# Element-wise work of the RWKV stages moved from GpSimd to ScalarE and VectorE in a two-layer trunk

## The chip, the cores and the metric

One NeuronCore of one Trainium2 chip. The metric is the device time of one execution, in microseconds. The kernel before takes 2108.77 us, the median of 3 runs (2105.18 to 2111.51).

## The reference

A trunk of two layers on 512 latent tokens and 256 context tokens, 1024 features, fp32. Layer 0 mixes by attention in four head pairs (MLA) and, on the other half of its width, by an RWKV-7 scan over the tokens, forwards and backwards, in 8 heads of 64. Layer 1 mixes by a gated linear recurrence. After each mixer comes a layer norm, a squared-ReLU MLP and another layer norm; all are modulated by the condition. The part that the change touches is the RWKV half:

```python
f = f + mu * (centred_shift(f) - f)          # centred_shift: half the sum of both neighbours
r, k, v, wl, al, gl = jnp.split(f, RWKV_SPLIT, axis=-1)
decay = jnp.exp(-jnp.exp(-softplus(-(w0 + tanh(wl) @ w2)) - 0.5))     # per direction
a = sigmoid(a0 + al @ a2)
kk = k * k_k;  kk = kk * rsqrt(sum(kk * kk) + 1e-12)                  # per head
k_dir = k * (1 + (a - 1) * k_a)
# per token: sa = S kk;  S = S * decay - sa (kk a)^T + v k_dir^T;  y = S r
```

## The kernel before

The program is written in pieces, and a planner orders the instructions of each engine by a simulated timeline when the program is built; on the chip each engine then runs its list in order. All DMAs that matter here go through SyncE's queue.

**Feature stage (`mixer0_in`, L963).** The modulated input lies feature-major in SBUF, as a high and a low part; a product with 128 columns of the input weights takes three matmuls per 128 rows, over the spans `SPANS` of 512 latent and 256 context tokens, into one of two banks `mm` (`product`, L1098). The weights come by DMA and are split into high and low part by ScalarE (L130) and VectorE (L136). Of the projections, three (decay, a and gate) go first, in banks of their own (`first`, L1134); then, for four head pairs p, one of k, of r and of v. Each goes through the token mix (`shift`, L1113): ScalarE copies each span into a padded row `fp` (L1127), VectorE adds the two neighbours (L1120), GpSimd scales the middle by `mu1` (L1121), VectorE combines both by `mu2` (L1124, twice). `keys` (L1196) makes the normalised key: GpSimd scales by `k_k` (L1199), ScalarE squares, TensorE sums over a head. `turn_v` (L1212) turns v token-major (L1218).

`features` (L1222) makes the operands of one head pair and direction: ScalarE's tanh of decay (L1226) and a (L1231); GpSimd scales the decay (L1232); VectorE's scan gives the log decay (L1236, L1238); ScalarE's exponentials `eq` and `ek` (L1242, L1243); GpSimd makes `kd` (L1247), times k (L1248); VectorE makes the rows of `pq` and `bk` (L1252 to L1254, L1268), GpSimd one more of `bk` (L1269) and one column of `pq` (L1255). Its `rest` (L1256) multiplies A of every 64-token chunk on TensorE (L1264), into the banks `z0` and `z1`, and VectorE masks it into `at` (L1265). After both directions, `inverse` (L993) copies both `at` to DRAM (L997), reads back the 16 x 16 diagonal blocks by 16 DMAs (L1004), inverts them on VectorE (L1010, L1012), and sends them back by DMA (L1018, L1022); GpSimd clears the diagonal blocks of `at` with `offm` (L1024). `series` (L1026) builds the whole inverse from both by products (L1040, L1055) and VectorE (L1045, L1057). `bonus` (L1274) is a side product.

**Pass over the chunks (`rwkv`, L1324).** 12 steps for each of four head pairs, both directions side by side. `prep` (L1339) loads the operands of four steps and multiplies all token pairs (L1367); the result is masked into `st`: half of it by VectorE out of the bank (L1371), the other half, but for the first group, by a ScalarE copy (L1373) and a GpSimd mask (L1374). A step (`step`, L1395) has two links: products into `z` (L1404, L1406), GpSimd scales the state `rv` by the decay into `ds` (L1412), VectorE overwrites it by a copy out of `z` (L1414); then products (L1424) and VectorE's new state (L1426), outputs (L1428) and ScalarE's copy of them (L1429). TensorE gets pieces of attention (`mla`, L765) between the links, 1.4 us of them planned for each.

Then come the output product, the MLP and layer 1, dense products all.

Of the kernel before, what the change touches and what calls it, by code (L numbers as in the profile page):

```python
# [10 lines left out]
F32 = mybir.dt.float32  # L11
# [7 lines left out]
NL = 512  # L19
# [8 lines left out]
def run(*gens):  # L28
    """emits pieces of work in turn"""
    gens = list(gens)  # L30
    while gens:
        gens = [g for g in gens if next(g, gens) is not gens]


def weave(tc, dense, lead):
    """emits pieces of both in turn; a dense piece is not issued before the piece of lead that it follows"""
    for ins in lead:
        with tc.issue_after(ins.ins):
            next(dense, None)
    run(dense)  # L40


class Rows:
    """[128, n, T] of several tiles"""
# [9 lines left out]
class Kern:  # L54
# [28 lines left out]
    def dense(self, stk, wbufs=(2, 3), mmb=4):  # L83
        """pools of the phases with dense products: PSUM, weights, small rows"""
# [13 lines left out]
    def rows(self, stk):  # L98
        """token-major rows"""
# [8 lines left out]
    # ---- parameter vectors as per-partition columns  # L108
# [29 lines left out]
    def fill(self, n=1):  # L138
        """emits up to n pieces of work that other phases left for later"""
# [4 lines left out]
    def paced(self, gen):  # L144
        """a piece of work that is not issued before the product that was emitted last"""
# [3 lines left out]
    # ---- weights: raw column groups, then hi/lo column tiles  # L149
# [5 lines left out]
    def w_split(self, raw, hi_eng="act", lo_eng="dve"):  # L155
        """raw [128, kt, c] -> (hi, lo)"""
# [6 lines left out]
    def w_tiles(self, ap, group=128, eng=("act", "dve")):  # L163
        """yields (j, (hi, lo)) for 128-column tiles of ap [K, M]"""
# [9 lines left out]
    def mm3(self, out, st, mv, ks, first=True, last=True):  # L174
        """out += sum_k st_k^T mv_k over (hi, lo) pairs; st(k), mv(k) -> (hi, lo) APs"""
# [12 lines left out]
    # ---- adaLN modulation: columns [128, 48, 2]  # L188
# [48 lines left out]
    def mods_spare(self, l, order, tag="md", raws=None, tmp=None):  # L237
        """the same for 128-column blocks, with buffers of its own: fills gaps of the tensor engine; yields after each"""
# [51 lines left out]
    # pieces of the modulation: 0 sh1, 1 sc1, 2 g1, 3 sh2, 4 sc2, 5 g2  # L290
# [3 lines left out]
    def scale1(self, l, piece, name):  # L294
        """1 + scale, [128, 8, 2]"""
# [9 lines left out]
    def ln_affine(self, l, lnname, shp, scp, mod_l, name):  # L305
        """columns for h = xn*G + B with the modulation (shp, scp) of layer mod_l folded in"""
# [19 lines left out]
    def ln_turn(self, t, i, end):  # L326
        """token-major rows of token tile i up to feature row end, and their statistics"""
# [8 lines left out]
    def ln_stats(self, t, i):  # L336
        """token tile i: rows in PSUM, mean and variance, 1 / deviation"""
# [12 lines left out]
    def ln_stats_norm(self, t, i):  # L350
        """token tile i: returns normalised [128 tok, 1024] in SBUF"""
# [47 lines left out]
    # ---- squared-ReLU MLP; accumulates (g/alpha) * mlp(h) into t  # L399
    def mlp(self, l, t, hhi, hlo, halves, g2, after_half):  # L400
# [3 lines left out]
        for ch in range(4):  # L404
# [3 lines left out]
            if ch == 0:  # L408
                # the first half, while the second is normalised
# [31 lines left out]
    def mm_residual(self, t, m, a, b, st, mv, ks, g, ps=None):  # L441
        """t[:, m, a:b] += g[m] * (st^T mv)"""
# [10 lines left out]
    # ---- last layer norm, token-major, straight to the output  # L453
# [11 lines left out]
    # ---- tokens in, feature-major out  # L465
# [1233 lines left out]
```

## Time and profile before

| | us |
|---|---|
| median of 3 runs (lowest, highest) | 2108.77 (2105.18, 2111.51) |
| the profiled execution: span, first to last instruction | 2108.1 |
| TensorE busy, share of the span | 1937.9, 92% |
| VectorE busy | 1286.0, 61% |
| ScalarE busy | 815.3, 39% |
| GpSimd busy | 449.6, 21% |
| mean granted TensorE clock | 0.962 |

The profile is of one execution. A time of an engine counts only what it executes, not what it waits; a wait is put down to the instruction that ended last among those waited for. In the rows, PE is TensorE, PEld its weight loads, DVE VectorE, ACT ScalarE, POOL GpSimd; L12 is a line of the kernel, and buffer numbers are left out of the names. The granted clock is a share of full speed. Matmul durations overlap: one can start before the one ahead of it has ended.

### The profile page before, as it was taken

The page shows a single profiled execution, that of the slowest core. Times are in us where ns is not written, and L with a number is a line of the kernel's source. Part 1 is how long each engine was busy: PE and PEld are TensorE (multiplying, and loading weights), DVE is VectorE, ACT ScalarE, POOL GpSimd, SP SyncE. Part 2 cuts the span into 40 slices and gives each one's busy share as a digit, 9 for nine tenths or more (in the row PEclk, how much of TensorE's full clock was granted, in tenths as well). Part 3 has the DMA queues.
Part 4 walks back from the last instruction along what each step waited for, and adds up shares of the span by engine and source line. Part 5 has one row for each costly group of instructions (what it writes and reads, how often), then busy time and mean ns, then how long its engine had stood idle before and what let it go on. Part 6 is the DMA issues. An engine that isn't in the chain of part 4 may idle for free.

```text
span 2108.1 us, 39763 instructions
## 1 busy us (share of the span) xinstructions
PE 1937.9 (92%) x16130; PEld 1734.2 (82%) x16130; DVE 1286.0 (61%) x2524; ACT 815.3 (39%) x1413; POOL 449.6 (21%) x473
## 2 busy tenths in 40 slices
PE   7888788699999988999999999999978889999997
PEld 4666666577777768999999999998867779999997
DVE  4558767737666668774654333456799665444456
ACT  2344232434545443441231321334768444233242
POOL 0346544624535531000000000001244200000000
PEclk8999899789999998999999999999989999999999
DMA  9455534544423228332332222246421673333334
GB/s 345 131 172 180 139 107 128 174 121 117 124 64 92 77 72 243 91 90 80 100 87 84 61 60 61 69 126 179 112 71 45 182 219 97 94 95 96 100 101 141
DMA packets 429302, 249.19 MB, mean 118 GB/s; under 512 B 79376, under 2 KB 414144, under 8 KB 428992
## 3 DMA queue, kind: packets, MB, share of 16 engines
q1 hardware_dynamic: 428648, 245.55, 39.7%
q8 instruction: 127, 2.08, 0.4%
q0 software_dynamic: 288, 1.05, 0.1%
q14 instruction: 55, 0.45, 0.1%
q10 hardware_dynamic: 184, 0.06, 0.0%
HBM read 209.38 MB, written 36.44 MB: 117 GB/s over the span
## 4 chain that ended last, share of the span: by engine, by line
PE 66%; DVE 13%; DMA 7%; ACT 4%; issue 4%; SPq 3%; POOL 2%; DVEq 0%; ACTq 0%; POOLq 0%
PE mm L183 16%; PE mm L184 16%; PE mm L185 16%; SPq L1004 2%; DVE wlo L136 2%; PE tr L183 2%; DMA wraw<-in_l_mlp_w_dram 1%; PE tr L184 1%; PE tr L185 1%; PE mm L884 1%; PE g L1390 1%; PE mm L875 1%; ACT whi L130 1%; POOL fp L1121 1%; PE g L1367 1%
## 5 line engine op out<-in xcount | busy, mean ns | idle before, releaser
L183 PE MATMUL mm<-hhi,whi 128*128 128x384 f32 (+2 forms) x1504 | 489.4, 326 | 2.0 <-DVE msq L427 2.0
L184 PE MATMUL mm<-hlo,whi 128*128 128x384 f32 (+2 forms) x1504 | 485.0, 323 | 0.2 <-DVE hlo L396 0.2
L185 PE MATMUL mm<-hhi,wlo 128*128 128x384 f32 (+2 forms) x1504 | 484.5, 322 | 0.0
L130 ACT CAST whi<-wraw 128x1024 fp32r<-128x1024 f32 x216 | 226.3, 1049 | 552.5 <-PE mm L184 452.5
L183 PE MATMUL mm<-uhi,whi 128*128 128x384 f32 (+1 forms) x1280 | 400.4, 314 | 3.5 <-DVE t L450 3.0
L185 PE MATMUL mm<-uhi,wlo 128*128 128x384 f32 (+1 forms) x1280 | 399.8, 313 | 2.8 <-DVE wlo L136 2.8
L136 DVE TENSOR_TENSOR wlo<-wraw,whi 128x1024 fp32r<-128x1024 f32 x216 | 277.4, 1285 | 203.6 <-ACT whi L130 199.2
L184 PE MATMUL mm<-ulo,whi 128*128 128x384 f32 (+1 forms) x1280 | 399.0, 312 | 1.8 <-DVE ulo L136 1.8
L183 PEld LDWEIGHTS mm<-hhi,whi 128*128 128x128 f32 x1504 | 285.4, 190 | 15.6 <-issue 2.7
L184 PEld LDWEIGHTS mm<-hlo,whi 128*128 128x128 f32 x1504 | 285.2, 190 | 10.5 <-issue 0.8
L185 PEld LDWEIGHTS mm<-hhi,wlo 128*128 128x128 f32 x1504 | 284.8, 189 | 10.1
L183 PEld LDWEIGHTS mm<-uhi,whi 128*128 128x128 f32 x1280 | 244.7, 191 | 4.9 <-DVE t L450 3.2
L185 PEld LDWEIGHTS mm<-uhi,wlo 128*128 128x128 f32 x1280 | 244.2, 191 | 4.5 <-DVE wlo L136 4.1
L184 PEld LDWEIGHTS mm<-ulo,whi 128*128 128x128 f32 x1280 | 244.4, 191 | 2.6 <-DVE ulo L136 2.3
L450 DVE SCALAR_TENSOR_TENSOR t<-mm,g,t 128x256 f32<-128x256 f32 (+2 forms) x200 | 93.0, 481 | 224.7 <-PE mm L185 220.7
L347 POOL TENSOR_TENSOR lnrs<-lnrs,mhalf 128x1 f32<-128x1 f32 x20 | 10.8, 546 | 1005.1 <-DVE lnrs L346 1005.0
L1412 POOL TENSOR_SCALAR ds<-rv,rw_dd 64x64 f32<-64x64 f32 x176 | 84.3, 479 | 160.6 <-DVE rv L1426 150.6
L427 DVE SCALAR_TENSOR_TENSOR msq<-mm,mr 128x384 f32<-128x384 f32 (+1 forms) x128 | 62.4, 487 | 45.0 <-ACT mr L425 44.8
L425 ACT ACTIVATE mr<-mm 128x384 f32<-128x384 f32 (+1 forms) x128 | 55.5, 434 | 83.7 <-PE mm L185 83.7
L130 ACT CAST uhi<-msq 128x384 fp32r<-128x384 f32 (+1 forms) x128 | 58.6, 458 | 75.1 <-DVE msq L427 74.9
L136 DVE TENSOR_TENSOR ulo<-msq,uhi 128x384 fp32r<-128x384 f32 (+1 forms) x128 | 63.3, 495 | 32.3 <-ACT uhi L130 28.6
L1426 DVE SCALAR_TENSOR_TENSOR rv<-z,rw_dd,ds 64x64 f32<-64x64 f32 x176 | 49.6, 282 | 28.1 <-PE z L1424 23.3
(416 smaller groups left out, 3087.4 us busy)
## 6 DMA issues: line engine op xcount, KB each, us to landing
wraw<-in_l_mlp_w_dram SPq DMA_DIRECT2D x148, 512.0 KB
mraw<-in_l_mod_w_dram SPq DMA_DIRECT2D x48, 512.0 KB
wraw<-in_l_w_in_dram SPq DMA_DIRECT2D x36, 512.0 KB
wraw<-in_l_w_out_dram SPq DMA_DIRECT2D x32, 512.0 KB
mw<-in_l_mod_w_dram SPq DMA_DIRECT2D x16, 512.0 KB
wraw<-in_l_mod_w_dram SPq DMA_DIRECT2D x16, 512.0 KB
rw_bk<-pqbk SPq DMA_DIRECT2D x8, 768.0 KB
rw_pq<-pqbk SPq DMA_DIRECT2D x8, 768.0 KB
```

The source lines that it names most:

```text
L130: nc.scalar.copy(hi, src)
L136: e.tensor_tensor(out=lo, in0=src, in1=hi.bitcast(F32), op=ALU.subtract)
L183: nc.tensor.matmul(out, sh, mh, start=f, stop=False)
L184: nc.tensor.matmul(out, sh, ml, start=False, stop=False)
L185: ins = nc.tensor.matmul(out, sl, mh, start=False, stop=l)
L425: nc.scalar.activation(r, ps, AF.Relu)
L427: nc.vector.scalar_tensor_tensor(out=sq, in0=ps, scalar=0.0, in1=r, op0=ALU.max, op1=ALU.mult)
L450: nc.vector.scalar_tensor_tensor(out=t[:, m, x:y], in0=ps[:, x - a:y - a], scalar=g[:, m, s:s + 1], in1=t[:, m, x:y], op0=ALU.mult, op1=AL ...
L875: nc.tensor.transpose(ps[:, j * 128:(j + 1) * 128], p[:, (j0 + j) * 128:(j0 + j + 1) * 128], self.ident)
L1004: nc.sync.dma_start((X, tm)[d][q:q + 45:4, e], dat[r0:r0 + 16, 12 * d:12 * d + 12, 16 * b:16 * b + 16].rearrange("s n t -> n s t"))
L1412: P.tensor_scalar(out=ds[d][H[e]], in0=rv[H[e], i, e, :], scalar1=dn[H[e]], scalar2=None, op0=ALU.mult)
L1426: V.scalar_tensor_tensor(out=rn[H[e], e, :], in0=zu[d][H[e], 1], scalar=dn[H[e]], in1=ds[d][H[e]], op0=ALU.mult, op1=ALU.add)
```

## The change

- Token mix: ScalarE scales each span by `mu1` on its way out of the bank; VectorE then adds each neighbour out of the bank, one product-and-add per neighbour and span. The padded rows and GpSimd's scaling are gone.
- A: VectorE writes two masked copies out of the bank: `dg` (all of the triangle, for the copy to DRAM) and `at` (the off-diagonal blocks alone). GpSimd's mask is gone; the constant `offmask` now holds the sign and the triangle of each direction.
- The scalings of the key (`k_k`) and of `kd` go from GpSimd to ScalarE, the decay's scaling, the key product and one row of `bk` from GpSimd to VectorE.
- In the pass, all of the pair products are masked by VectorE out of the bank, and the state is scaled by ScalarE.
- Some small tiles share one, and three constants live in another pool.

```diff
-    off = (s // 16) != (t // 16)
+    off = np.stack([((s // 16) != (t // 16)) * np.where(m, -1.0, 0.0) for m in (s > t, t > s)], 1)
...
-        offm = cload(self.c0, self.C["offmask"], [128, 64], "offm")
+        goff = cload(self.tmp, self.C["offmask"], [128, 2, 64], "goff")
...
-            for d, at in enumerate(ats):
-                nc.sync.dma_start(dat[:, 12 * d:12 * d + 12], at)
+            for d, (_, dg) in enumerate(ats):
+                nc.sync.dma_start(dat[:, 12 * d:12 * d + 12], dg)
...
-            for at in ats:
-                P.tensor_tensor(out=at, in0=at, in1=offm.unsqueeze(1).to_broadcast([128, 12, 64]), op=ALU.mult)
...
-                    V.tensor_tensor(out=s[:, 0:FW - 2], in0=fp[:, 0:FW - 2], in1=fp[:, 2:FW], op=ALU.add)
-                    P.tensor_scalar(out=fp[:, 1:FW - 1], in0=fp[:, 1:FW - 1], scalar1=mu1[:, j:j + 1], scalar2=None, op0=ALU.mult)
-                    for a, b in SPANS:
-                        o = a + (2 if a else 0)
-                        V.scalar_tensor_tensor(out=out[:, a:b], in0=s[:, o:o + b - a], scalar=mu2[:, j:j + 1],
-                                               in1=fp[:, o + 1:o + 1 + b - a], op0=ALU.mult, op1=ALU.add)
+                def evac(ps, a, b):
+                    A.activation(out[:, a:b], ps, AF.Copy, scale=mu1[:, j:j + 1])
+                    n = b - a
+                    for o, i in ((1, 0), (0, 1)):
+                        V.scalar_tensor_tensor(out=out[:, a + o:b - i], in0=ps[:, i:n - o], scalar=mu2[:, j:j + 1],
+                                               in1=out[:, a + o:b - i], op0=ALU.mult, op1=ALU.add)
...
-                P.tensor_scalar(out=kx, in0=f, scalar1=cols["l0_rwkv_k_k"][:, p:p + 1], scalar2=None, op0=ALU.mult)
+                A.activation(kx, f, AF.Copy, scale=cols["l0_rwkv_k_k"][:, p:p + 1])
...
-                P.tensor_scalar(out=lamp[:, 1:T + 1], in0=lamp[:, 1:T + 1], scalar1=CDEC, scalar2=CDEC, op0=ALU.mult, op1=ALU.add)
+                V.tensor_scalar(out=lamp[:, 1:T + 1], in0=lamp[:, 1:T + 1], scalar1=CDEC, scalar2=CDEC, op0=ALU.mult, op1=ALU.add)
...
-                P.tensor_scalar(out=kd, in0=ta, scalar1=kah[:, p:p + 1], scalar2=kam[:, p:p + 1], op0=ALU.mult, op1=ALU.add)
-                P.tensor_tensor(out=kd, in0=kd, in1=k, op=ALU.mult)
+                A.activation(kd, ta, AF.Identity, scale=kah[:, p:p + 1], bias=kam[:, p:p + 1])
+                V.tensor_tensor(out=kd, in0=kd, in1=k, op=ALU.mult)
...
-                    at = isb("at", (128, 12, 64), 4)
+                    at, dg = isb("at", (128, 12, 64), 4), sb("dg", (128, 12, 64), 2)
...
-                        V.tensor_tensor(out=at[:, 6 * i:6 * i + 6], in0=ps, in1=gmask[:, d:d + 1, :].to_broadcast([128, 6, 64]), op=ALU.mult)
-                    return at
+                        for x, m in ((dg, gmask), (at, goff)):
+                            V.tensor_tensor(out=x[:, 6 * i:6 * i + 6], in0=ps, in1=m[:, d:d + 1, :].to_broadcast([128, 6, 64]), op=ALU.mult)
+                    return at, dg
...
-                P.tensor_tensor(out=bk[:, :, 1, :], in0=ch(kd), in1=ch(ek), op=ALU.mult)
+                V.tensor_tensor(out=bk[:, :, 1, :], in0=ch(kd), in1=ch(ek), op=ALU.mult)
...
-                if e or p + j == 0:
-                    V.tensor_tensor(out=st[h, :, e], in0=kp[h], in1=mk, op=ALU.mult)
-                else:
-                    A.copy(st[h, :, e], kp[h])
-                    P.tensor_tensor(out=st[h, :, e], in0=st[h, :, e], in1=mk, op=ALU.mult)
+                V.tensor_tensor(out=st[h, :, e], in0=kp[h], in1=mk, op=ALU.mult)
...
-                        P.tensor_scalar(out=ds[d][H[e]], in0=rv[H[e], i, e, :], scalar1=dn[H[e]], scalar2=None, op0=ALU.mult)
+                        A.activation(ds[d][H[e]], rv[H[e], i, e, :], AF.Copy, scale=dn[H[e]])
```

## Rows read from the trace of the kernel before

**Rows 1.** Stages: us, busy PE, PEld, DVE, ACT, POOL, granted clock, DMA share, GB/s.

```profile
50.00:430.00 380.00, 312.38 (x2984) 246.44 (x2984) 257.07 (x418) 143.12 (x242) 192.38 (x137) 0.91 0.50 145
...
430.00:770.00 340.00, 324.61 (x4140) 248.68 (x4142) 218.58 (x613) 163.39 (x406) 144.86 (x228) 0.99 0.34 95
...
820.00:2108.00 1288.00, 1227.30 (x8484) 1184.36 (x8482) 745.07 (x1330) 474.54 (x701) 98.34 (x78) 0.98 0.36 103
```

**Rows 2.** TensorE's waits from 50 to 430 us: total, times, longest.

```profile
PE g L1055 <- DVE vt L1057: 6.8, 5, 2.8
...
PE z L1424 <- ACT bt L1392: 4.3, 3, 2.8
```

**Rows 3.** TensorE's timeline: start, us, instruction, idle before and its releaser.

```profile
216.19 1.09 PE L1218 MATMUL mm<-ident,f_v 128*128 128x128 f32 x4 [8.25 <-ACT ek L1243]
...
284.55 0.87 PE L1218 MATMUL mm<-ident,f_v 128*128 128x128 f32 x3 [7.11 <-DVE f_v L1124]
...
353.13 1.12 PE L1264 MATMUL z<-pqbk,pqbk 64*64 64x64 f32 x16 [4.86 <-POOL pqbk L1255]
```

**Rows 4.** VectorE: two lines' durations (min/median/max ns), and its timeline.

```profile
L1254 DVE TENSOR_TENSOR pqbk<-f_kk,eq x8: 930/2554/2597, 122.0 to 350.4; 128x756 f32<-128x756 f32 x8
...
L136 DVE TENSOR_TENSOR wlo<-wraw,whi x216: 1193/1226/2884, 26.1 to 2093.0; 128x1024 fp32r<-128x1024 f32 x108
...
215.30 1.14 DVE L1124 SCALAR_TENSOR_TENSOR f_v<-sh,mu,fp 128x512 f32<-128x512 f32 x2
```

**Rows 5.** Timeline of GpSimd and ScalarE: start, us, instruction, idle before.

```profile
278.22 5.40 POOL L1121 TENSOR_SCALAR fp<-fp,mu 128x770 f32<-128x770 f32 x1 [3.19 <-DVE sh L1120]
...
338.96 0.48 ACT L1231 ACTIVATE ta<-z,a0h 128x256 f32<-128x256 f32 x1 [0.18 <-PE z L1175]
...
342.64 3.43 POOL L1024 TENSOR_TENSOR at<-at,ri_offm 128x768 f32<-128x768 f32 x1 [8.54 <-DMA dat<-at]
...
346.07 0.97 POOL L1247 TENSOR_SCALAR kd<-ta,kah,kam 128x768 f32<-128x768 f32 x1
```

**Rows 6.** GpSimd's groups by line: busy us, mean ns, idle before.

```profile
L1412 POOL TENSOR_SCALAR ds<-rv,rw_dd 64x64 f32<-64x64 f32 x176 | 84.3, 479 | 160.6 <-DVE rv L1426 150.6
...
L1121 POOL TENSOR_SCALAR fp<-fp,mu 128x770 f32<-128x770 f32 x15 | 43.2, 2880 | 55.2 <-DVE sh L1120 53.7 <-DVE modred L232 1.4
...
L1374 POOL TENSOR_TENSOR st<-st,gmask 64x512 f32<-64x512 f32 x22 | 28.6, 1305 | 22.5 <-ACT st L1373 21.4
```

**Rows 7.** Groups of VectorE and ScalarE that price what moves.

```profile
L1371 DVE TENSOR_TENSOR st<-g,gmask 64x512 f32<-64x512 f32 x26 | 17.7, 682 | 4.7 <-ACT st L1373 3.9
...
L1265 DVE TENSOR_TENSOR at<-z,ri_gmask 128x384 f32<-128x384 f32 x16 | 8.7, 551 | 2.8 <-PE z L1264 2.6
...
L754 DVE TENSOR_TENSOR ek<-ek,eq 128x768 f32<-128x768 f32 x2 | 1.9, 955 | 1.4 <-ACT ek L750 1.4
...
L1188 DVE TENSOR_SCALAR ta<-ta 128x768 f32<-128x768 f32 x1 | 0.6, 556 | 0.0
...
L1429 ACT COPY ys<-z 128x64 f32<-128x64 f32 x96 | 20.2, 216 | 46.5 <-PE z L1428 42.5 <-DVE p L865 1.8 <-DVE bt L1379 1.4
...
L1373 ACT COPY st<-g 64x512 f32<-64x512 f32 x22 | 12.8, 581 | 11.6 <-PE g L1367 5.7 <-issue 2.2 <-POOL st L1374 1.4
...
L1226 ACT ACTIVATE lamp<-tr,w0h 128x768 f32<-128x768 f32 x8 | 7.2, 904 | 3.1 <-PE tr L1175 3.1
...
L1242 ACT ACTIVATE eq<-ek 128x768 f32<-128x768 f32 x8 | 6.8, 846 | 29.1 <-DVE ek L1238 17.8 <-DVE ek L1236 11.3
```

**Rows 8.** The stage table again, for four short windows.

```profile
210.00:220.00 10.00, 3.78 (x11) 2.97 (x12) 9.84 (x13) 5.09 (x10) 7.43 (x3) 0.55 0.43 129
...
280.00:290.00 10.00, 4.73 (x15) 3.70 (x16) 8.76 (x10) 5.57 (x11) 9.05 (x5) 0.52 0.31 54
...
350.00:360.00 10.00, 6.16 (x54) 4.67 (x55) 7.56 (x8) 4.42 (x7) 6.07 (x4) 0.55 0.59 127
...
394.00:430.00 36.00, 25.68 (x203) 19.67 (x205) 26.90 (x64) 11.03 (x25) 24.23 (x34) 0.65 0.70 195
```

More of the change, by code (lines that the diff above doesn't have):

```diff
@@ L980, in cload @@
         def cload(pool, src, shape, name):
-            t = pool.tile(shape, F32, name="ri_" + name)
+            t = pool.tile(shape, F32, name="ri_" + name, bufs=1)
             nc.sync.dma_start(t, src)
@@ L1022, in inverse @@
                         nc.sync.dma_start(dst[r0:r0 + 16, :, 16 * b:16 * b + 16], dx[e, :, b].rearrange("n s t -> s n t"))
-            for at in ats:
-                P.tensor_tensor(out=at, in0=at, in1=offm.unsqueeze(1).to_broadcast([128, 12, 64]), op=ALU.mult)
         def series(p, ats):
+            ats = [at for at, _ in ats]
             vts = [isb("vt", (128, 12, 64), 2) for d in range(2)]
@@ L1068, in mixer0_in @@
             col = lambda n, name: ri.tile([128, n], F32, name=name)
-            mu1, mu2, eps = col(15, "mu1"), col(15, "mu2"), col(1, "kkeps")
+            small = col(56, "small")
+            mu1, mu2, w0h, a0h, kah, kam, eps = (small[:, a:b] for a, b in zip((0, 15, 30, 38, 46, 50, 54), (15, 30, 38, 46, 50, 54, 55)))
             V.tensor_scalar(out=mu1, in0=mu, scalar1=-1.0, scalar2=1.0, op0=ALU.mult, op1=ALU.add)
@@ L1077, in mixer0_in @@
             V.tensor_scalar(out=kam, in0=kah, scalar1=-1.0, scalar2=1.0, op0=ALU.mult, op1=ALU.add)
-            fps = [col(FW, f"fp{i}") for i in range(2)]
-            for fp in fps:
-                for a, n in ((0, 1), (NL + 1, 2), (FW - 1, 1)):
-                    P.memset(fp[:, a:a + n], 0.0)
             lamp = col(T + 2, "lamp")
@@ L1086, in mixer0_in @@
             low = {n: [ri.tile([128, T], F32R, name=f"x{n}{d}") for d in range(2)] for n in ("w2", "a2")}
-            sh = lambda: sb("sh", (128, FW), 2)
+            sh = lambda: sb("sh", (128, T), 2)
             def wide(mm):
@@ L1113, in shift @@
             def shift(j, out):
-                fp = fps[nt[0] % 2]
-                nt[0] += 1
-                def mix():
-                    s = sh()
-                    V.tensor_tensor(out=s[:, 0:FW - 2], in0=fp[:, 0:FW - 2], in1=fp[:, 2:FW], op=ALU.add)
-                    P.tensor_scalar(out=fp[:, 1:FW - 1], in0=fp[:, 1:FW - 1], scalar1=mu1[:, j:j + 1], scalar2=None, op0=ALU.mult)
-                    for a, b in SPANS:
-                        o = a + (2 if a else 0)
-                        V.scalar_tensor_tensor(out=out[:, a:b], in0=s[:, o:o + b - a], scalar=mu2[:, j:j + 1],
-                                               in1=fp[:, o + 1:o + 1 + b - a], op0=ALU.mult, op1=ALU.add)
-                return (lambda ps, a, b: A.copy(fp[:, a + 1 + (2 if a else 0):b + 1 + (2 if a else 0)], ps)), mix
+                def evac(ps, a, b):
[4 more added lines that the diff above has]
+                                               in1=out[:, a + o:b - i], op0=ALU.mult, op1=ALU.add)
+                return evac
             def project(j, out):
-                evac, mix = shift(j, out)
-                yield from product(self.w_raw(w[:, W0 + 128 * j:W0 + 128 * j + 128], 8, 128), evac)
-                mix()
+                yield from product(self.w_raw(w[:, W0 + 128 * j:W0 + 128 * j + 128], 8, 128), shift(j, out))
             def first(js, outs):
@@ L1143, in first @@
                             self.mm3(o, lambda k: (wh[:, k, :], wl[:, k, :]), lambda k: (hhi[:, k, a:b], hlo[:, k, a:b]), [k], k == 0, k == 7)
-                for (evac, mix), pp in zip(after, ps):
+                for evac, pp in zip(after, ps):
                     for o, (a, b) in zip(pp, SPANS):
                         evac(o, a, b)
-                    mix()
                     yield
```

7 lines of the change are left out of this document (3 added, 4 removed).

## The prediction

> **What bounds the kernel now.** First the stretches [rows 1]. TensorE works 324.6 of the 340 us in which attention and the pass over the chunks run together, and 1227.3 of the last 1288 us, the dense layers that the change leaves alone. In the feature stage (50 to 430 us) it works 312.4 of 380 us: 67.6 us idle, 17.8%, at a granted clock of 0.91. GpSimd is busy 192.4 us there, VectorE 257.1. So a change to element-wise work can pay in that stage alone; in the pass, TensorE's idle share is 15.4 of 340, 4.5%.
>
> Next, which waits ended last for TensorE there [rows 2, 3]. Three gaps stand out. At 216.19 the transposes of v (L1218) start after 8.25 us, at 284.55 after 7.11 us, and at 353.13 the products for A (L1264) after 4.86 us. The rest are waits for the series (L1055) and for the first steps of the pass (L1424).
>
> Then what stood behind them. In the first two, v comes out of the token mix: VectorE adds the neighbours, GpSimd scales (L1121), VectorE combines (L1124). At 278.22 GpSimd took 5.40 us over the scaling, where L1121 needs 2.88 on average [rows 5, 6], and v followed it. For the first gap the row names ScalarE, but v's combination started at 215.30 [rows 4], which ends where the transposes begin: I read v as the releaser. In the third, ScalarE had the tanh for k's scaling ready at 339.44 (338.96 + 0.48), but GpSimd, which works in order, was held by the off-diagonal mask of the previous A (L1024) until the copy of that A to DRAM let go at 342.64; the mask ended at 346.07, and only then came kd (L1247), the key product and the decayed key [rows 5]. That is 6.6 us lost in one queue.
>
> The two engines also slow each other. L1254, the same VectorE product eight times, takes 930 ns at best and 2554 ns as median; the split of the weights (L136) 1226 ns as median and up to 2884 [rows 4].
>
> **The change, part by part.** TensorE's work is the same, and no DMA is added or taken away: the copy to DRAM reads the diagonal copy of A from a tile of its own. So the sum is over TensorE's idle time and its clock.
>
> *Token mix.* For each of 15 projections one GpSimd scaling (2880 ns, 43.2 us in all [rows 6]) and one VectorE addition go; ScalarE scales as it empties the bank, and VectorE adds each neighbour out of the bank. VectorE keeps about the same load: one SBUF addition and two combinations become four half-length combinations; a 512-column one out of PSUM should cost 0.68 us, as L1371 does [rows 7]. What goes is the hop to GpSimd and back. First gap: 8.25 us; the scaling's 3 us and the contention in front of it go, but the next weights still have to be split before the next projection, so I take 5.0 (bounds 0 and 8.25). Second gap: 7.11 us, of which GpSimd's 5.40 went wholly into the wait; I take 4.8 (bounds 0 and 7.11).
>
> *Masks of A, scalings and key products.* kd moves to ScalarE (0.90 us, as L1226 with a column operand), and the wait behind the DRAM copy is gone: 6.6 us in that chain against a gap of 4.86. I take 4.2 (bounds 0 and 4.86). The first key scaling (L1199) also goes to ScalarE, 4 passes at 0.85 to 0.90; it lies beside other work, and without that cover costs at most 3.6 us.
>
> *The clock after the gaps.* In the 10 us windows around the three gaps the granted clock was 0.55, 0.52 and 0.55 [rows 8], between the levels of 2.4 and 1.2 GHz; a mean of 0.55 puts 0.9 of the time at the lower one. That costs half of 0.9 x 3.78, 0.96 x 4.73 and 0.9 x 6.16 us of busy time: 1.7, 2.3 and 2.8, together 6.8. With the gaps cut to about a third, I take 4.5 back.
>
> *The start of the pass.* From 394 to 430 us TensorE is idle 10.3 us, at clock 0.65, with GpSimd busy 24.2 of 36 [rows 8]. The mask of the pair products (L1374) and the state scaling (L1412) leave GpSimd; the copies of the shared key and of the weights stay. I take half of the idle time, 5 (bounds 0 and 10.3, and up to 9 of clock: 0.7 x 25.68 / 2).
>
> *What VectorE pays.* New on it in the feature stage: 8 decay scalings at 0.556 us (L1188) = 4.4; 16 products at 0.955 (L754) = 15.3; 16 second masks at 0.551 (L1265) = 8.8; together 28.5 [rows 7]. Back come at least four L1254 at 2554 - 930 ns = 6.5. Net at most 22 us on an engine that is busy 257 of 380. Where this lands I can't see; weighted with TensorE's idle share it costs 22 x 0.178 = 3.9 (bounds 0 and 22).
>
> *The bank held longer.* No row shows a bank that waits for VectorE after a projection. Before, ScalarE alone emptied it; now two VectorE passes follow, 2 x 0.68 us plus their place in VectorE's queue. There are two banks, and the other one's products run meanwhile. Nearest is the feature stage's own idle share, so I take 1.5 us in all; bounds 0, and 36 (second rival).
>
> *The pass.* 176 state scalings (L1412, 84.3 us) leave GpSimd for ScalarE at about 0.216 us, the 128x64 copy's price: 38.0. 22 copies (L1373) at 0.581 go: 12.8. Net +25.2 on ScalarE; VectorE gains 22 masks at 0.682 = 15.0 and GpSimd loses 112.9 [rows 6, 7]. What queues behind a waiting scaling on ScalarE are the exponentials and copies of attention; TensorE waits for those. At TensorE's idle share of 4.5% the 40.2 us cost 1.8 (bounds -3, as the scalings were on the chain of steps too, and 8).
> The rows have 846 ns for a ScalarE pass with constants (L1242) and 904 for one with a column operand (L1226), equally long [rows 7]. The Trainium skill, *ScalarE: Activation LUTs*, section *What ACT_TABLE_LOAD costs*, puts 186 ns + 0.833 ns per element on a pass and about 93 ns on each column operand. The trace agrees in direction, with 58 ns. An estimate by that page is 332 ns for a scaling: 45.6 us net on ScalarE instead of 25.2, and 2.7 us in place of 1.8.
>
> **Sum.** -5.0 - 4.8 - 4.2 - 4.5 - 5.0 + 3.9 + 1.5 + 1.8 = -16.3 us. The profiled execution's span is 2108.1 us; the median of three runs is 2108.77, and the span lies within 0.7 of it. 2108.77 - 16.3 = 2092.5; I say **2092**.
>
> **The rivals.**
> A, *larger gain* (20%): the three gaps close wholly (20.2), their clock comes back (6.8), and the start of the pass loses its idle time and its low clock (19.3): 46 us, 2062. For it: the whole of the feature chain speeds up where both engines block each other now. Against: the inverse's many small DMAs and the series on VectorE stay, and fixed dates follow from them.
>
> B, *the hop goes, the time does not* (15%): VectorE becomes the bound of the feature stage. It is busy 9.84 and 8.76 of 10 us in the first two gap windows [rows 8]; with 22 us more, v's combination waits behind splits and masks instead of behind GpSimd. The gains of 23.5 are paid back by the 22 us: about 2107. The change then does what it says, and the gaps keep their length under another name.
>
> C, *slower* (12%): the two projection banks wait for VectorE. Three projections go first, in banks of their own; 12 remain, with two spans each: 24 evacuations. If a bank comes free 1.5 us too late each time, that is 36 us; -16.3 - 1.5 + 36 = +18, 2127. It decides from about 0.7 us each (16.3 + 1.5 over 24). For it: VectorE's queue is that full in [rows 8], and TensorE issues in order, so a late bank holds everything. Against: in these windows VectorE was full because of slowed instructions and of waits for GpSimd, which go.
>
> **How the numbers follow.** My forecast has 53%, A 20%, B 15%, C 12%. About 0.3%, 6.3 us, is what a measurement of this kernel tells from no change. Forecast and A are faster: 0.73; B is the same: 0.15; C slower: 0.12. The range, 2060 to 2114, takes in A and B and leaves out C's full price and what lies beyond A. The forecast alone, with the bounds of its gap terms, spans about 2078 to 2104.
>
> **What the changed profile would show.** Right: from 50 to 430 us GpSimd is busy under 149 us (192.4 less L1121's 43.2 alone), TensorE's idle time there is down by some 15 us, the wait of L1218 for v is a few us in all, and no wait of L1264 names a GpSimd product of 5 us; the pass begins some 15 us earlier and is as long as before. VectorE's L1254 sits near 0.93 us. Wrong: projections that wait for a VectorE addition (C); VectorE above 280 us in the stage with the gaps still there (B); or a pass longer than before with ScalarE named ahead of VectorE's state copies, which would put the cost of the state scalings far above my 1.8.

## The result and the profile after

The changed kernel takes 2123.59 us, the median of 8 runs (2116.98 to 2126.77), against 2109.77 for the kernel before, run beside it: a ratio of 1.0065, with a 95% interval of [1.0047, 1.0082]. One of the eight executions of the kernel before took 3421.4 us and is left out. The changed kernel is slower, where the prediction said 2092 and faster. The profiled execution (span 2115.9 us, mean granted clock 0.953) is one of its quicker ones, at 2117.68 us.

What was meant to go went. The stage table of the changed kernel (columns as in [rows 1]):

```profile
50.00:430.00 380.00, 316.24 (x3028) 250.06 (x3026) 248.02 (x475) 159.89 (x265) 50.82 (x61) 0.88 0.50 145
430.00:770.00 340.00, 316.51 (x3940) 243.06 (x3940) 219.96 (x599) 192.24 (x510) 44.70 (x54) 0.96 0.35 99
```

GpSimd's 192.4 us of the feature stage became 50.8, and VectorE, which got more to do, is busy 9 us less. But TensorE's idle time there fell by 3.9 us only (67.6 to 63.8), and its clock fell from 0.91 to 0.88. In the pass TensorE's busy time went down and its clock too. Four finer stretches show where, first of the kernel before, then of the changed one:

```profile
50.00:200.00 150.00, 134.70 (x889) 103.76 (x888) 93.51 (x136) 62.81 (x105) 71.71 (x40) 0.99 0.54 169
200.00:300.00 100.00, 76.67 (x841) 62.16 (x840) 77.62 (x132) 31.67 (x57) 56.52 (x32) 0.88 0.43 119
300.00:440.00 140.00, 111.00 (x1411) 88.62 (x1406) 88.77 (x161) 51.09 (x88) 65.91 (x69) 0.84 0.49 133
440.00:780.00 340.00, 322.03 (x4087) 245.53 (x4082) 222.83 (x628) 164.50 (x416) 145.74 (x230) 0.99 0.33 93
```

```profile
50.00:200.00 150.00, 128.27 (x807) 98.18 (x806) 87.49 (x157) 63.14 (x100) 7.67 (x12) 0.91 0.50 156
200.00:300.00 100.00, 91.77 (x896) 72.24 (x894) 77.84 (x160) 48.56 (x81) 10.48 (x13) 0.93 0.50 144
300.00:440.00 140.00, 106.20 (x1453) 87.72 (x1453) 86.71 (x169) 53.15 (x98) 34.15 (x42) 0.82 0.49 132
440.00:780.00 340.00, 315.01 (x3906) 241.53 (x3907) 222.20 (x607) 195.88 (x521) 43.22 (x48) 0.96 0.35 97
```

Width less PE busy is the idle time. From 200 to 300 us it fell from 23.3 to 8.2 us: both gaps of [rows 3] that lie there closed, and TensorE does not wait for the transposes of v in these 100 us. From 50 to 200 us it rose from 15.3 to 21.7 and the clock fell from 0.99 to 0.91; from 300 to 440 us it rose from 29.0 to 33.8; in the pass from 18.0 to 25.0, with the clock from 0.99 to 0.96. Over the 730 us that is 85.6 before and 88.7 after. Busy time times (1 - clock), a rough price of the lower level, makes 32 us before and 50 after (28 and 37 of these to 440 us).

TensorE's longest waits of the changed kernel from 50 to 430 us (total, times, longest):

```profile
PE g L1039 <- DVE vt L1044: 12.2, 3, 5.2
PE mm L1205 <- DVE f_k L1114: 7.1, 1, 7.1
PE mm L1039 <- DMA tau<-dx: 6.3, 1, 6.3
```

The first row is the series, which waited before too [rows 2]; the third is the last inverse's transfer. L1205 is the transposing of v, L1218 before. It does not wait for v now: it waits for f_k, another projection, whose bank it needs. VectorE's timeline around it, and TensorE's row:

```profile
177.22 0.74 DVE L1114 SCALAR_TENSOR_TENSOR f_k<-mm,small,f_k 128x511 f32<-128x511 f32 x1
179.50 0.61 DVE L1006 COPY X<-tm 48x512 f32<-48x512 f32 x1 [1.54 <-DMA tm<-dat]
180.14 1.76 DVE L1223 TENSOR_TENSOR_SCAN ek<-lamp,ri_reset 128x768 f32<-128x768 f32 x1
181.81 0.73 DVE L1114 SCALAR_TENSOR_TENSOR f_k<-mm,small,f_k 128x511 f32<-128x511 f32 x1
```

```profile
182.69 0.88 PE L1205 MATMUL mm<-ident,f_v 128*128 128x128 f32 x3 [7.08 <-DVE f_k L1114]
```

The first neighbour is added at 177.22. The second stands in VectorE's order behind the copy that opens the inverse (L1006), which waits for a DMA until 179.50, and behind a scan. From the end of the first addition (177.96) to the start of the second are 3.85 us, of which VectorE idles 1.54 for the DMA; the rest is the copy and the scan. The bank comes free at 182.54 (181.81 + 0.73), and 0.15 us later TensorE goes on, after 7.08 us. From 180 to 185 us its granted clock is 0.50, the level of 1.2 GHz, and 0.52 from 185 to 190. It is 0.50 as well from 320 to 325 us, after the series' longest wait (5.2), and from 420 to 430, after the wait for the transfer (6.3).

The pass starts earlier and lasts longer. The copies of its outputs, first and last start (before; after):

```profile
L1429 ACT COPY ys<-z x96: 191/212/253, 420.4 to 785.2; 128x64 f32<-128x64 f32 x96
```

```profile
L1413 ACT COPY ys<-z x96: 188/213/246, 409.6 to 801.5; 128x64 f32<-128x64 f32 x96
```

So 364.8 us became 391.9. The first eight copies alone take 60.1 us where they took 43.3 (the ninth starts at 469.7; before, at 463.7): the lead of 10.8 us is gone there. In these 60.1 us lie TensorE's 6.3 us of waiting for the last inverse's transfer (tau). The output product starts at 814.05 in place of 795.10. Of these 19 us, 11 come back by the end of this execution; where, was not followed.

Another price that was far off, that of the state scaling (first and last start again):

```profile
L1396 ACT ACTIVATE ds<-rv,rw_dd x176: 333/344/357, 402.6 to 792.4; 64x64 f32<-64x64 f32 x176
```

The state scaling takes 345 ns as a mean (60.7 us in 176), not the 216 of the copy row in [rows 7].
The estimate by the Trainium skill, *ScalarE: Activation LUTs*, section *What ACT_TABLE_LOAD costs*, was 332 ns; this row agrees with it within 4%.

### The profile page after: what moved, and what is told of

The parts are those of the page before. It is cut to its first block, busy times and chain, and to the rows that moved or that the text cites. A ratio compares the mean times of both kernels' runs of the same rounds, so it can differ in the third digit from the quotient of the medians.

```text
span 2115.9 us, 39567 instructions
## 1 busy us (share of the span) xinstructions
PE 1941.6 (92%) x16130; PEld 1738.2 (82%) x16130; DVE 1287.3 (61%) x2601; ACT 876.0 (41%) x1579; POOL 205.8 (10%) x210
## 4 chain that ended last, share of the span: by engine, by line
PE 66%; DVE 14%; DMA 6%; ACT 5%; issue 5%; SPq 3%; POOL 0%; DVEq 0%; ACTq 0%; POOLq 0%
PE mm L183 17%; PE mm L184 17%; PE mm L185 16%; DVE wlo L136 3%; SPq L1004 2%; DMA wraw<-in_l_w_out_dram 1%; PE tr L183 1%; DVE cy L592 1%; PE mm L875 1%; DMA wraw<-in_l_mlp_w_dram 1%; PE tr L185 1%; PE mm L884 1%; PE tr L184 1%; ACT whi L130 1%; DVE gx L644 1%
## 5 line engine op out<-in xcount | busy, mean ns | idle before, releaser
L184 PEld LDWEIGHTS mm<-hlo,whi 128*128 128x128 f32 x1504 | 287.3, 191 | 10.8 <-DVE hlo L396 0.5
L347 POOL TENSOR_TENSOR lnrs<-lnrs,mhalf 128x1 f32<-128x1 f32 x20 | 10.8, 548 | 996.6 <-DVE lnrs L346 961.2
L1396 ACT ACTIVATE ds<-rv,rw_dd 64x64 f32<-64x64 f32 x176 | 60.7, 345 | 25.8 <-DVE rv L1410 22.4
L276 DVE SCALAR_TENSOR_TENSOR macc<-mraw,sc,macc 128x128 f32<-128x128 f32 x224 | 67.6, 360 | 0.0
```

The source lines that it names most:

```text
L184: nc.tensor.matmul(out, sh, ml, start=False, stop=False)
L276: V.scalar_tensor_tensor(out=a, in0=raw[:, k], scalar=self.sc[:, k, i:i + 1], in1=a, op0=ALU.mult, op1=ALU.add)
L1396: A.activation(ds[d][H[e]], rv[H[e], i, e, :], AF.Copy, scale=dn[H[e]])
```

## The experiments

Each ratio is to the kernel before, run beside it on the same chip; the brackets are its 95% interval. "Feature edits" are the token mix, the masks of A, the scalings and the key products; "pass edits" are the state scalings on ScalarE and the pair masks on VectorE.

### Which half of the change

Four kernels undo or isolate the pass edits. The first has the feature edits alone:

```diff
-  A.activation(ds[d][H[e]], rv[H[e], i, e, :], AF.Copy, scale=dn[H[e]])
+  P.tensor_scalar(out=ds[d][H[e]], in0=rv[H[e], i, e, :], scalar1=dn[H[e]], scalar2=None, op0=ALU.mult)
...
-  V.tensor_tensor(out=st[h, :, e], in0=kp[h], in1=mk, op=ALU.mult)
+  if e or p + j == 0:
+      V.tensor_tensor(out=st[h, :, e], in0=kp[h], in1=mk, op=ALU.mult)
+  else:
+      A.copy(st[h, :, e], kp[h])
+      P.tensor_tensor(out=st[h, :, e], in0=st[h, :, e], in1=mk, op=ALU.mult)
```

> The changed kernel with both edits of the pass undone (state scalings on GpSimd, half of the pair products masked by GpSimd after a ScalarE copy); the feature stage stays changed. Theory P (the pass lost the time: 403.6 us from its first to its last state product where it was 382.2): the pass is back at 380 to 385 us and the whole runs 4 to 10 us below the kernel before. Theory F (the feature stage's new order and the banks held by VectorE lost it, and the pass only inherits a bad start): the whole stays 8 us or more above the kernel before.

Measured: 1.0073 [1.0046, 1.0100], median 2117.9 us; its profiled execution, at 2111.38, is its quickest one.

The changed kernel with the first replacement alone (state scalings back on GpSimd):

> The changed kernel with the state scalings alone back on GpSimd. Theory P1 (the scalings on ScalarE are what stretches the pass, 176 of them at 345 ns in a queue that attention waits for): the pass is below 387 us and the whole within 5 us of the kernel before, or below it. Theory P2 (the masks that moved to VectorE stretch it): the pass stays near 400 us and the whole 10 us or more above the kernel before.

Measured: 1.0046 [1.0028, 1.0064].

The changed kernel with the second replacement alone (pair masks back):

> The changed kernel with the masks of the pair products alone back on ScalarE and GpSimd. P1: the pass stays near 400 us, the whole 10 us or more above the kernel before. P2: the pass is below 387 us and the whole within 5 us of the kernel before, or below it.

Measured: 1.0071 [1.0051, 1.0092].

The kernel before with both pass edits and none of the feature edits:

> The kernel before with the two edits of the pass alone. P: the pass takes 395 to 405 us and the whole runs 13 to 22 us above the kernel before. F: the pass is at 385 us or less and the whole within 5 us of the kernel before.

Measured: 1.0087 [1.0064, 1.0110].

Neither half is innocent: the feature edits alone lose as much as the whole (theory F), and so do the pass edits alone (theory P). P1 and P2 both miss: either pass edit taken back leaves the pass about as long. The two losses do not add up in the changed kernel (0.73% + 0.87% against 0.65%). The length of the pass, from its first to its last state product, does not add up either: 382.2 us before, 398.2 with the feature edits alone, 401.8 with the pass edits alone, 403.7 with all; 399.3 and 402.2 with the scalings or the masks back.

### Is it only the planner's order?

Every edit makes the planner order each engine's list anew, so the order of the kernel before might just be a lucky one. Two kernels leave the work of before as it is and alter a number of the weave between pass and attention:

```diff
-                LINK = 1.4
+                LINK = 1.45
```

> The kernel before, with not one instruction of its work changed: only the weave of the pass is set a little otherwise (1.45 us of the attention's dense work let in per link of the pass in place of 1.40), so the planner writes another order of the same work. Theory O (order): every edit so far ran 0.5 to 0.9% longer because it makes the planner order the pass anew, and the weave's numbers fit one order only, that of the kernel before; then this kernel loses as well, 1.003 to 1.009 of before, its pass 395 to 404 us where before has 382, its output product starting at 805 to 815 us where before has 795. Theory W (work): what the edits put on ScalarE and VectorE makes the pass and the clock worse; then nothing is lost here, 0.998 to 1.002, pass 380 to 385 us.

Measured: 1.0001 [0.9982, 1.0019]; copies of ys from 422.5 to 787.0 us.

```diff
-                PRE = 21
+                PRE = 23
```

> Again the kernel before with its work as it was: 23 us in place of 21 us of dense work are let in ahead of the pass, the weave else unchanged. Theory O: 1.003 to 1.009 of before, pass 390 to 402 us. Theory W: 0.998 to 1.002, pass 378 to 385 us.

Measured: 1.0014 [0.9997, 1.0031]; copies from 421.4 to 790.7, so its pass is some us longer than theory W gave. And the changed kernel with PRE = 24:

> The changed kernel with 24 us in place of 21 us of dense work ahead of the pass. The feature stage ends its last inverse 11 us earlier than before, and the pass's first steps run slowly there (60 us for the first eight state copies, 43 before). Theory O: the numbers of the weave no longer fit; another number moves the time by several us in either direction, 0.998 to 1.008 of before, where the changed kernel had 1.0065. Theory W: the edits' work sets the time, so it stays within 0.15% of 1.0065.

Measured: 1.0110 [1.0086, 1.0135]. Theory O falls for the kernel before: another order of the same work cost it 0.01% and 0.14%, where it asked for 0.3% or more. For the changed kernel it is theory W that missed: it asked for 0.15% at most, and this one step moved it by 0.45%. Differences of that size between its variants are not to be read as the price of an edit.

### The token mix alone

```diff
...
-   return (lambda ps, a, b: A.copy(fp[:, a + 1 + (2 if a else 0):b + 1 + (2 if a else 0)], ps)), mix
+   def evac(ps, a, b):
+       A.activation(out[:, a:b], ps, AF.Copy, scale=mu1[:, j:j + 1])
+       n = b - a
+       for o, i in ((1, 0), (0, 1)):
+           V.scalar_tensor_tensor(out=out[:, a + o:b - i], in0=ps[:, i:n - o], scalar=mu2[:, j:j + 1],
+                                  in1=out[:, a + o:b - i], op0=ALU.mult, op1=ALU.add)
...
```

> The kernel before with one edit of the change: the token mix reads its projection out of PSUM (ScalarE's scaled copy, then two additions on VectorE), everything else as before. Theory O: the gaps in the feature stage shrink by 3 to 5 us, the pass is ordered anew and grows by 10 to 20 us: 1.002 to 1.008. Theory W, with the projection banks held by VectorE: 1.002 to 1.005 too, but with the loss ahead of the pass, that is the first state copies of the pass later than before's 420 us and the pass as long as before's 382 us.

Measured: 1.0133 [1.0106, 1.0159], worse than either theory gave and worse than any other kernel here. The loss lies ahead of the pass: its copies run from 437.5 to 809.7 us, 372.2 us long but 17 us late. Some of TensorE's waits from 50 to 440 us in it:

```profile
PE mm L1040 <- DMA tau<-dx: 17.5, 2, 15.9
PE g L1055 <- DVE vt L1057: 6.2, 1, 6.2
...
PE mm L183 <- DVE f_v L1115: 4.3, 1, 4.3
PE mm L1206 <- DVE f_k L1115: 3.0, 1, 3.0
```

The wait on f_k's bank is there again (3.0 us), a projection waits for f_v's (4.3 us), and the largest wait is now that for the last inverse's transfer.

### Who empties the bank

The feature edits alone, with one alteration: ScalarE writes the bank out twice, and VectorE adds from the second copy, in SBUF.

```diff
...
+    s = box[0]
     A.activation(out[:, a:b], ps, AF.Copy, scale=mu1[:, j:j + 1])
+    A.activation(s[:, a:b], ps, AF.Copy, scale=mu2[:, j:j + 1])
     n = b - a
     for o, i in ((1, 0), (0, 1)):
-        V.scalar_tensor_tensor(out=out[:, a + o:b - i], in0=ps[:, i:n - o], scalar=mu2[:, j:j + 1],
-                               in1=out[:, a + o:b - i], op0=ALU.mult, op1=ALU.add)
+        V.tensor_tensor(out=out[:, a + o:b - i], in0=out[:, a + o:b - i], in1=s[:, a + i:b - o], op=ALU.add)
```

> The feature-stage edits alone (1.0073 of before), with one thing altered: the projection's bank is emptied by ScalarE alone, which writes it twice, scaled by either weight; the two additions on VectorE read the copy. Theory B (bank): in the feature edits a bank is held until VectorE's second addition, which in its order stands behind a wait for the inverse's DMA and behind a scan; the transposes of v wait 5.5 us for it at 175.4 us and the clock falls to 1.2 GHz for the next 10 us. Then this wait goes, TensorE's idle time from 50 to 200 us falls from 20.5 to about 15 us and the ratio to 0.997 to 1.003. Rival D (dates): the inverses' DMAs and VectorE's chains set the stage's dates, the wait is replaced by another behind the same chain: idle from 50 to 440 us stays within 4 us of 62 us and the ratio is 1.004 to 1.009.

Measured: 0.9925 [0.9895, 0.9955], median 2092.32 us (the profiled execution, 2083.01, is its quickest): the loss of 0.73% turned into a gain of 0.75%. The stretches of the feature edits alone, with the wait of L1205, then of this kernel, with its longest wait for ScalarE on a projection's bank:

```profile
50.00:200.00 150.00, 129.52 (x806) 99.30 (x805) 89.16 (x160) 62.80 (x99) 7.68 (x12) 0.90 0.50 157
200.00:300.00 100.00, 92.55 (x896) 72.27 (x895) 76.21 (x158) 49.05 (x82) 11.22 (x13) 0.93 0.50 144
300.00:440.00 140.00, 105.75 (x1428) 86.45 (x1428) 84.48 (x161) 49.52 (x84) 41.99 (x56) 0.83 0.49 132
...
PE mm L1205 <- DVE f_k L1114: 5.5, 1, 5.5
```

```profile
50.00:200.00 150.00, 139.04 (x907) 108.06 (x906) 93.98 (x173) 85.43 (x143) 7.66 (x14) 0.98 0.55 171
200.00:300.00 100.00, 84.24 (x915) 67.63 (x914) 76.71 (x152) 43.31 (x74) 13.73 (x13) 0.85 0.49 133
300.00:440.00 140.00, 119.85 (x1683) 97.32 (x1685) 90.00 (x192) 53.69 (x94) 50.33 (x67) 0.90 0.53 146
...
PE mm L1210 <- ACT f_k L720: 3.2, 1, 3.2
```

TensorE idles 11.0, 15.8 and 20.2 us, 46.9 in all to 440 us, against 67.6 before, 63.8 in the changed kernel and 62.2 with the feature edits alone, with the clock back at 0.98 ahead of 200 us. The pass is as long as before and starts 19.8 us earlier:

```profile
L1422 ACT COPY ys<-z x96: 201/213/253, 400.6 to 766.7; 128x64 f32<-128x64 f32 x96
```

ScalarE pays 23 us more ahead of 200 us (85.43 against 62.80). VectorE's additions get hardly cheaper: of 511 columns they take 0.69 us out of SBUF against 0.74 out of PSUM. Rival D falls, and theory B has the direction; the gain is larger than the 0.997 to 1.003 that it gave. The wait that went was 5.5 us, and the profiled executions lie 28 us apart. What shows beside the wait is 15.3 us less idle time in all to 440 us, no wait for the last inverse's transfer above 0.7 us (6.4 with the bank on VectorE), and a pass of 381.7 us in place of 398.2; how the one grows out of the other was not followed.

The same feature edits with VectorE's wait for the DMA given away instead:

```diff
-  V.tensor_copy(X[64:112].rearrange("p e j i -> p e i j"), tm[64:112])
+  P.tensor_copy(X[64:112].rearrange("p e j i -> p e i j"), tm[64:112])
```

> The feature-stage edits alone, with the copy that opens each inverse (48 partitions x 512, 0.61 us on VectorE, which waits there for the DMA tm<-dat, 16.1 us over four in the changed kernel) given to GpSimd, which has little left to do. Theory B, in the form that VectorE's wait for the DMA is what holds the bank: L1205's wait falls from 5.5 us to under 3 us, ratio 0.998 to 1.004. Rival D: 1.004 to 1.009.

Measured: 1.0016 [0.9995, 1.0038], and the wait of L1205 on f_k is 3.5 us: the two additions now lie 1.6 us apart in place of 3.7, with the scan still between them. So taking the copy and its wait out of VectorE's list brings 0.57% back; taking the bank off VectorE brought 1.48%.

The whole change, with the bank emptied by ScalarE:

> The changed kernel whole, with only the emptying of the projection's bank altered (ScalarE writes it twice, VectorE adds from the copy). Theory B + S (the held bank costs in the feature stage, the pass edits cost in the pass, each by itself): between 0.9925 (no pass edit) and 0.9925 + 0.0042 + 0.0039 = 1.0006; forecast 0.998. Rival: the loss of the whole change is in how its parts meet, so the whole stays above 1.003.

Measured: 1.0006 [0.9989, 1.0023], which is 0.9925 and the two pass edits, one by one below, added up. So the rival falls; the forecast was 0.998. The pass is 398.9 us long here: with the bank free, the pass edits alone make it longer.

The kernel before with the token mix alone, bank emptied by ScalarE:

> The kernel before with the token mix alone, its bank emptied by ScalarE, scaled by either weight, the additions on VectorE from the copy. Theory B: the mix alone out of PSUM had 1.0133, and the bank's holder is all that is altered, so 0.993 to 1.003, TensorE's wait for the last inverse's transfer (17.5 us there) falls under 8 us. Rival: the mix alone is slow because the rest of the stage still stands on GpSimd: 1.008 to 1.014.

Measured: 1.0055 [1.0032, 1.0078]. It lies between what theory B and its rival gave. The bank was 0.8% of 1.3%; the rest is not explained by it. In this kernel TensorE waits 6.8 us for tau (17.5 with the bank held), 9.4 us at the products for A behind their operands, and 8.2 us once ahead of the pass behind VectorE's work on an inverse (L1010). The operands' chain still runs over GpSimd here; whether that sets the 9.4 us was not tested.

Both the bank by ScalarE and the opening copy by GpSimd:

> The feature edits with the bank emptied by ScalarE and, besides, the inverse's opening copy on GpSimd. With the bank gone from VectorE, its wait for the DMA holds nothing that TensorE asks for soon, so by theory B little is added: 0.990 to 0.995. If VectorE's waits still set the stage's dates: under 0.990.

Measured: 0.9980 [0.9963, 0.9997], 0.55% slower than without the second. The guess was wrong: with the bank free, giving that copy to GpSimd did not help. The difference is little more than the 0.45% of the other weave above, and it was not followed.

The best kernel with another weave (PRE = 23):

> The feature edits with the bank emptied by ScalarE (0.9925 of before), its work as it was, with 23 us in place of 21 us of dense work let in ahead of the pass. If the gain comes from the bank and the hop over GpSimd: 0.990 to 0.996. If it hangs on one order of the planner: 0.997 to 1.003.

Measured: 0.9941 [0.9926, 0.9956]. The gain does not hang on one order: this one moved it by 0.16%.

The kernel before with only the scalings and products:

> The kernel before with only the feature stage's scalings on ScalarE and its key products and the decay's scaling on VectorE; token mix, masks and pass as before, so the bank is emptied by ScalarE. The prediction's sum puts the third gap and the contention's end on it, some 5 to 8 us: 0.996 to 0.999. If the hop over GpSimd in these chains was not on the path: 0.999 to 1.004.

Measured: 0.9989 [0.9969, 1.0009]: at most a small gain, on the border of the two forecasts. Neither the token mix nor these edits gain by themselves (the masks of A were not run alone); all together, with the bank off VectorE, they do.

### The pass edits one by one

The kernel before with the state scalings on ScalarE alone:

> The kernel before with one edit: the state scalings on ScalarE. Theory S: eight of them in a row take 2.9 us of ScalarE at a boundary of four steps (8 x 0.345 us), the copies of ys stand behind them, and the next step's first product waits for its bank; each such wait drops TensorE's clock to 1.2 GHz for the next 5 to 10 us. The scalings alone then carry most of the loss of both pass edits (1.0087): 1.004 to 1.009, a wait of 2 to 3 us on ys near 705 us. Rival M (masks): the loss of the pass edits comes from VectorE, which takes the masks: 0.998 to 1.003 here.

Measured: 1.0042 [1.0024, 1.0059]. And with the pair masks on VectorE alone:

> The kernel before with one edit: all masks of the chunk products on VectorE out of PSUM. Theory S: 0.997 to 1.002. Rival M: 1.004 to 1.009, with TensorE waiting more for VectorE's state copies (6.2 + 2.8 us from 440 to 780 us before).

Measured: 1.0039 [1.0017, 1.0061]. Both cost, so neither theory holds as it was put: S had the masks at nothing, M the scalings. M's sign did not come either: with the masks alone TensorE waits 5.2 and 1.5 us for VectorE's state copies from 440 to 780 us, against 6.2 and 2.8 before. S also forecast a wait of 2 to 3 us on ys near 705 us with the scalings alone; it was 0.7 us there. With both edits that wait is there. ScalarE's timeline in the changed kernel, and TensorE's row:

```profile
704.82 2.94 ACT L1396 ACTIVATE ds<-rv,rw_dd 64x64 f32<-64x64 f32 x8
707.78 0.37 ACT L888 COPY ao<-mm 128x256 f32<-128x256 f32 x1
708.05 0.33 ACT L1413 COPY ys<-z 128x64 f32<-128x64 f32 x2
```

```profile
708.32 0.34 PE L1388 MATMUL z<-rv,st 128*64 128x64 f32 x4 [2.63 <-ACT ys L1413]
```

Eight scalings in a row, 2.94 us, stand ahead of the copies of ys, and the next step's first product needs the bank that these empty. Windows of the changed kernel around it:

```profile
700.00:704.00 4.00, 4.00 (x44) 2.59 (x42) 1.56 (x6) 0.90 (x2) 0.00 (x0) 1.00 0.22 54
704.00:708.00 4.00, 1.69 (x19) 1.00 (x15) 0.42 (x1) 3.76 (x11) 0.00 (x0) 1.00 0.11 33
708.00:712.00 4.00, 3.58 (x34) 2.61 (x34) 2.86 (x11) 2.17 (x9) 0.00 (x0) 0.58 0.01 2
712.00:716.00 4.00, 4.00 (x27) 3.00 (x28) 2.36 (x10) 1.27 (x5) 0.00 (x0) 0.50 0.10 31
716.00:720.00 4.00, 4.00 (x18) 3.09 (x18) 0.00 (x0) 0.78 (x2) 0.00 (x0) 0.64 0.35 101
```

TensorE was fully busy at 2.4 GHz, stood still 2.6 us, and then ran at or near 1.2 GHz for some 10 us: busy time times (1 - clock) is 1.5 + 2.0 + 1.4 = 4.9 us, an estimate of what came on top of the 2.6. Neighbouring products of 256 columns show it: they start 0.12 us apart ahead of the wait and 0.21 behind it.

```profile
705.08 0.28 PE L184 MATMUL tr<-kx0l,qh 128*128 128x256 f32 x1
705.20 0.28 PE L185 MATMUL tr<-kx0h,ql 128*128 128x256 f32 x1
...
709.69 0.41 PE L184 MATMUL tr<-kx1l,qh 128*128 128x256 f32 x1
709.90 0.41 PE L185 MATMUL tr<-kx1h,ql 128*128 128x256 f32 x1
```

The same wait of 2.6 us, on the same copies, stands in the kernel with the pass edits alone and in the whole change with the bank emptied by ScalarE.
The Trainium skill, *TensorE: Matmul & The Clock Gate*, section *HAM oscillation — how this bites in real kernels*, describes a kernel whose products wait for DMAs between bursts, where each next burst starts at 1.2 GHz, at a price of half the time spent there; the rows above agree, though the wait here is one for ScalarE. Where either pass edit alone loses its 0.4% stays open. With the scalings alone the pass is no longer than before (381.4 us; 382.2), and the longest wait on ys in it is 0.8 us; TensorE waits 5.6 us for the state copies (L1414) where it waited 2.8. With the masks alone the pass takes 392.2 us, and one product of the operands' preparation waits 2.6 us for VectorE, behind an instruction of the modulation (L257).

## Why the prediction was wrong

**The term that failed is "the bank held longer", 1.5 us.** It was priced by the stage's idle share, as no row showed a bank that waits for VectorE, and the larger price was left to rival C with 12%. C named the mechanism: two projection banks wait for VectorE while TensorE issues in order. What C had wrong was the form. Not 24 evacuations came late by 1.5 us each; the named waits on these banks are one of 7.1 us, with the second addition behind a copy that waits for a DMA and behind a scan, and two on f_r, 2.4 us together. The bank by ScalarE is worth 1.48% on the feature edits (1.0073 to 0.9925), some 31 us, and 0.59% on the whole change (1.0065 to 1.0006), some 12 us; on the token mix alone it is 0.78%. The waits named are a third of the 31 us at most, and the way from them to the rest was not followed. The argument against C, that slowed instructions and waits for GpSimd would go, was right about these (VectorE is busy 9 us less) and left out VectorE's wait for DMAs: the opening copies wait 16.1 us over four, where one waited 5.5 before.

The changed kernel lies 1.40% (1.0065 to 0.9925), some 30 us, above the one without pass edits and with the bank emptied by ScalarE, and that is nearly all of the 31.6 us by which the forecast was off. The prediction had 3.3 us for both terms. How the 1.40% splits depends on which is undone first: 0.59% for the bank and then 0.81% for the pass edits, or 1.48% for the bank with the pass edits gone already, and undoing those first gave nothing back (1.0065 to 1.0073). That the kernel without both, at 2092.32 us, meets the forecast of 2092 is in part luck, as the other terms did not come out one by one either.

**The gaps closed, and by more than forecast.** The first two were to give 9.8 us; idle time from 200 to 300 us, the whole window and not the gaps alone, fell by 15.1. No wait of the products for A on GpSimd is left, as the third term said, but its 4.2 us do not show: idle time from 300 to 440 us rose by 4.8.

**The clock went the other way.** 4.5 us were to come back after the gaps. From 50 to 430 us the granted clock fell from 0.91 to 0.88: it is 0.50 in the 5 us windows behind the waits of 7.1, 5.2 and 6.3 us.

**The start of the pass.** It begins 10.8 us earlier, where the sum wanted some 15, and its first eight outputs then take 16.8 us longer. With the bank emptied by ScalarE it begins 19.8 us earlier and keeps that.

**VectorE's load, 3.9 us, was not a loss.** The prices were right (masks of A 554 and 549 ns, decay scaling 558, key product 955; the addition out of PSUM 0.74 us at 177.22 against 0.68), but the end of the contention gave back more than was counted: L1254's product takes 939 ns in place of a mean of 1958 (L1241 now), as the prediction said it would, and the scan of one direction 1757 ns in place of a mean of 2558 (that of the other took 1742 before already). The trace of the kernel before shows beside what the product was slow. Five of eight took 2.55 to 2.60 us, and each started within 0.9 us of GpSimd's start on the row of `bk` that the change moved away (L1269):

```profile
184.16 2.58 DVE L1254 TENSOR_TENSOR pqbk<-f_kk,eq 128x756 f32<-128x756 f32 x1
...
183.38 2.55 POOL L1269 TENSOR_TENSOR pqbk<-kd,ek 128x768 f32<-128x768 f32 x1
```

The Trainium skill, *GPSIMD Engine Reference*, section *1. Specifications*, has GpSimd share its SBUF interfaces with VectorE's instructions of two SBUF inputs; that product has two, and agrees.

**The pass, 1.8 us, was mis-sized.** The two edits cost 0.42% and 0.39% by themselves, some 9 and 8 us, and 0.87% together. The scaling was priced by a copy row (216 ns; measured 345), and its cost by an idle share of 4.5%. That share knows nothing of order: eight scalings in a row ahead of a bank's release cost 2.6 us at once and the clock behind it. This one wait is shown; it is not the whole 18 us, and the scalings alone lose without it. The prediction gave a longer pass with ScalarE named as the sign of its own error. With both edits the pass is longer by 20 us; with the scalings alone it is not.

**The rivals.** B does not hold: VectorE did not become the bound, as it is busy 248 us of the stage and not above 280. The "fixed dates" that speak against A do not decide, since the pass came 20 us earlier once the bank was free; A's gain was not reached by any kernel. Two of the prediction's sums are off by some us. B with all of its terms gives 2110.6 (2092.5 + 22 - 3.9), not 2107; and with no gain at all from gaps, clock and start the forecast ends at 2116 (2092.5 + 23.5), not 2104. The measured time lies above both.

**What stays open:** why the losses of the two halves, and what either adds to the length of the pass, do not add in the changed kernel while they do with the bank free; how waits on banks of some 8 to 10 us become up to 31; why the token mix alone costs 0.55% even then; and where each pass edit alone loses.

## What to carry to other kernels

Before an evacuation moves from an engine with slack to a busy one, read what stands in that engine's list between the bank's last product and its last reader, above all instructions that wait for DMAs: an average load says nothing of it. Leaving the bank to the engine with slack, even to be read twice, and doing the arithmetic from SBUF can be cheaper; here that turned 1.0065 into 1.0006 and, with the pass left as it was, into 0.9925. Where TensorE is busy 95%, as in this pass, taking work off an engine with slack brought nothing, and a stall was paid again at the lower clock.

## What the runs showed of the hardware

A stall of 2.6 us in a stretch that was full at 2.4 GHz was followed by about 10 us at or near 1.2 GHz, so by estimate it cost about 7.5 us and not 2.6. A VectorE product of two SBUF operands (L1254 before) took 2.55 to 2.60 us the five times that it started within 0.9 us behind the start of a GpSimd product (L1269), and 0.93 to 0.95 the other three. One of these three started 3.2 us into a GpSimd product, and that one took 6.70 us in place of some 2.6. A ScalarE pass of 64x64 with a column operand out of SBUF takes 345 ns where a 128x64 copy out of PSUM takes 213, with as many elements per partition; whether the source or the column operand makes the difference was not separated.
